# Attention planned with zero-padded key and query stacks, value products of two query tiles, and four fixed pairs of accumulator banks

## The chip, the cores and the metric

The kernel runs on one core of a Trainium2 chip, one launch, inputs and outputs in device memory. The metric is the device time of one execution in microseconds (us). PE is TensorE (PEld its weight loads), DVE VectorE, ACT ScalarE, POOL GpSimd, SP the queue that issues most transfers. PSUM, where matmuls write, has 8 banks of 512 fp32 columns.

## What is computed

Two transformer-like layers over 512 latent and 128 context tokens, model width 1024. A layer is a modulated RMSNorm, one input projection, three groups of heads side by side (a bidirectional RG-LRU, grouped-query attention "G" with 8 heads, differential attention "D" with 4 heads), an output projection with a gated residual, then a second norm and a gated MLP with a width-3 convolution. The part that matters here:

```python
def _gqa_attend(q, k, v):                # 8 query heads, 2 key/value heads, head width 64
    s = einsum('bqhgd,bkhd->bhgqk', qblk, k) * scale
    p = softmax(s)                       # latent queries see 128 context + 512 latent keys
    return einsum('bhgqk,bkhd->bqhgd', p, v)

def _diff_attend(q, k, v, lam):          # 4 heads, two 32-wide components each
    s = einsum('bqhcd,bkhcd->bchqk', qblk, k) * scale
    p = softmax(s)
    att = p[:, 0] - lam * p[:, 1]
    return einsum('bhqk,bkhd->bqhd', att, v)
```

## The kernel before

Engines run their own instruction streams in program order, with semaphores between them; the order of each stream is fixed when the program is written out. Weights come in fp32 and are split into a rounded high part and a remainder (`split_next`: one ACT copy, one DVE subtraction); projections are three matmuls per tile (`mm3`, L344 to L346).

Two things set the order. `Flow` holds pieces of work by a time at which they become due and writes them out while matmuls go by. `Plan` writes out the attention stage of a layer: `plan_attention` makes a list of tasks with an engine, an assumed duration, a key, needs and counted rooms (3 score buffers `ps` of two banks, 2 single banks `pb`, 10 slots `tp`), and `Plan.run` steps a clock and writes the task with the smallest key that can start. Keys and the order of units come from the table `PLAN`, one entry per layer.

A layer's order: projections of q (`evac_gq`), of k, v and D's q (`evac_kvdq`), of D's k and v (`evac_dkdv`), then the two 128-wide tiles of the RG-LRU gate (`m` = 2 and 3, tiles `lacc`, L344 to L346 with 320 columns), then the plan. While the last ones run, `Flow` writes out context attention (`ctx_stage` L1034, `ctx_norm` L1056 to L1063, `ctx_T` L1071), the RG-LRU's gate product (L686) with its split `mix_out` (ACT L639, DVE L640), and the five stacks of D's first key pair.

A **stack** (`d_stack`) is what D's score matmul needs of one token tile: for four heads, high, high and low part side by side (3 x 32 = 96 columns). POOL rounds the high part (L349), DVE makes the low part (`lo`, L905), PE transposes it (`tr`, L910, tile `dT`), DVE copies it to `dks` or `dqs` in two halves (`out`, L914). A layer has 18: five keys and four queries for each of two head pairs. The plan writes 13, `d_stack_flow` the first five.

The plan's work for one unit (one head, 128 queries): scores on PE (L1147 and L1148 for G, L1152 for D), maximum on DVE (`nm`, L1158), exponential on ACT (L1162), reciprocal on DVE (L1167), scaling on POOL (L1173), for D a combination on DVE (L1177), transposes on PE (L1182, `PT`), their copy on ACT (L1187), and for every second unit the value product on PE (L1205, context part L1209, tile `PV`) with a copy on ACT (L1221). Between them PE runs the modulation products of later layers (`ada_gen`, L487), whose 1 MB of weights per piece SP loads. 48 units, 24 value products a layer.

`psum_mode` closes the PSUM pools of a stage and opens those of the next: 8 single banks outside the plan, 3 doubles and 2 singles in it.

Of the kernel before, what the change touches and what calls it, by code (L numbers as in the profile page):

```python
# [11 lines left out]
F32 = mybir.dt.float32  # L12
# [22 lines left out]
CX = (3000, 6500, 4000, 3000, 6000, 12000, 8000)  # L35
FIN = 7000
NP = (1250, 4000, 950, 1700)
PLAN = [dict(units="GDGDGGGGDGGGGDGGGDGGDDGGGDGGDGDDGGGGDDGGDDGGGGDG",
             G=(9, -21, 59, -142, -12, -22, 57, -93),
             D=(7, 28, 94, -471, 19, 10, -62, 241),  # L40
             ada=(131, -55, 4800), stacks=(2, 116, -14)),
        dict(units="GGGGGGDGGGDGGDGGDGDDGGGDGGDGGDGDDDGDGDGGGGDGDGGG",
             G=(-28, -30, -9, 36, -2, -50, 265, 122),
             D=(-18, 54, 54, -325, 3, -201, 99, -124),
             ada=(102, -48, 7800), stacks=(9, 164, 20))]
DT = 1500
# [47 lines left out]
class Plan:  # L94
# [3 lines left out]
    LAT = 180  # L98

    ROOM = dict(ps=3, pb=2, tp=10, sm=14, st=2, pt=5)  # L100

    def __init__(self, fl):
        self.fl, self.room, self.tasks = fl, dict(self.ROOM), []

    def task(self, eng, dur, key, fn, deps=(), take=None, give=None, cond=None, after=(), extra=()):
        t = dict(eng=eng, dur=dur, key=key, fn=fn, deps=list(deps), take=take or {}, give=give or {}, cond=cond,
                 after=list(after), extra=list(extra), end=None, n=len(self.tasks))
        self.tasks.append(t)
        return t

    def run(self):
        now, free, gifts = 0.0, {}, []
        left = sorted(self.tasks, key=lambda t: (t["key"], t["n"]))
        while left:
# [4 lines left out]
            started = False  # L119
            for t in left:  # L120
                if free.get(t["eng"], 0) > now:
                    continue
                if any(d["end"] is None or d["end"] + (0 if d["eng"] == t["eng"] else self.LAT) > now for d in t["deps"]):
                    continue
                if any(d["end"] is None or d["end"] + lag > now for d, lag in t["after"]):
                    continue
                if any(self.room[k] < n for k, n in t["take"].items()) or (t["cond"] and not t["cond"]()):
                    continue
                for k, n in t["take"].items():
# [1517 lines left out]
```

## Time and profile before

| | |
|---|---|
| median of 3 runs | 1640.56 us (1638.94 to 1643.58) |
| the profiled execution's own time | 1643.37 us |
| its span | 1641.6 us |
| PE busy, share of the span | 97% |
| DVE, ACT, POOL busy | 58%, 44%, 21% |
| scores of layer 0 start / first product after its attention | 179.81 / 306.18 us |
| the same in layer 1 | 984.92 / 1102.90 us |

Times in the trace are us from the start of the span. A row of the order of time gives start, duration and, in brackets, how long the engine was idle before it and what it waited for. The duration of a matmul row is longer than the distance to the next, because matmuls overlap in the engine; the distance between starts is what one costs.

### The profile page before, as it was taken

What the parts mean: (1) busy time and instruction counts of PE and PEld (TensorE: products, weight loads), DVE (VectorE), ACT (ScalarE), POOL (GpSimd) and SP (SyncE); (2) the same over time, 40 slices, a digit from 0 to 9 for tenths busy, and PEclk for the clock granted to TensorE, in tenths of its full rate; (3) what the DMA queues carried; (4) which work ended last, traced back from release to release, by engine and by line L of the source; (5) the groups of instructions that cost most, each with busy time, mean ns of one, the idle gap of its engine ahead of it and who ended that gap; (6) DMA issues with size and microseconds to landing.
All of it is one profiled execution on the core that took longest, in us unless ns stands there. A gap on an engine that the chain in (4) does not pass through costs nothing. (4 is left out here: it accounts for less than half of the span.)

```text
span 1641.6 us, 25381 instructions
## 1 busy us (share of the span) xinstructions
PE 1594.2 (97%) x10070; PEld 1393.8 (85%) x10070; DVE 945.0 (58%) x1548; ACT 726.3 (44%) x1500; POOL 344.8 (21%) x746
## 2 busy tenths in 40 slices
PE   6999899999999999999999999999999999999998
PEld 4778677789999889999887777777899998899986
DVE  5787777465555434555477777865655553355544
ACT  4745677634333212333247357884433331133331
POOL 5162233122111000110052513420411100011101
PEclk9999999999999999999999999999999999999999
DMA  9222465411313221222212214442112232121212
GB/s 331 69 86 78 142 218 208 156 52 53 102 52 108 98 77 52 78 78 90 90 41 71 75 58 155 136 162 102 52 52 86 69 129 78 52 78 54 101 65 90
DMA packets 99435, 161.04 MB, mean 98 GB/s; under 512 B 10670, under 2 KB 69222, under 8 KB 94196
## 3 DMA queue, kind: packets, MB, share of 16 engines
q1 hardware_dynamic: 98068, 158.00, 28.8%
q8 instruction: 79, 1.29, 0.3%
q0 software_dynamic: 1040, 1.14, 0.2%
q14 instruction: 40, 0.33, 0.1%
q10 hardware_dynamic: 208, 0.28, 0.0%
HBM read 155.95 MB, written 3.44 MB: 97 GB/s over the span
## 5 line engine op out<-in xcount | busy, mean ns | idle before, releaser
L330 DVE TENSOR_TENSOR wl<-raw,wh 128x1024 fp32r<-128x1024 f32 x180 | 219.9, 1227 | 410.1 <-ACT wh L329 409.1
L345 PE MATMUL uacc<-hl,wh 128*128 128x320 f32 (+2 forms) x1408 | 437.4, 311 | 0.8 <-DVE hl L574 0.5
L344 PE MATMUL uacc<-hh,wh 128*128 128x320 f32 (+2 forms) x1408 | 435.9, 310 | 0.0
L346 PE MATMUL uacc<-hh,wl 128*128 128x320 f32 (+2 forms) x1408 | 434.2, 308 | 0.2 <-DVE wl L330 0.2
L329 ACT ACTIVATE wh<-raw 128x1024 fp32r<-128x1024 f32 x180 | 189.6, 1059 | 180.3 <-PE tacc L346 148.6
L346 PEld LDWEIGHTS uacc<-hh,wl 128*128 128x128 f32 x1408 | 265.6, 189 | 0.7 <-DVE wl L330 0.7
L345 PEld LDWEIGHTS uacc<-hl,wh 128*128 128x128 f32 x1408 | 264.5, 188 | 1.7 <-DVE hl L574 1.6
L344 PEld LDWEIGHTS uacc<-hh,wh 128*128 128x128 f32 x1408 | 264.7, 188 | 0.3
L344 PE MATMUL tacc<-wh,g 128*128 128x512 f32 x440 | 174.2, 396 | 0.0
L345 PE MATMUL tacc<-wl,g 128*128 128x512 f32 x440 | 173.8, 395 | 0.0
L346 PE MATMUL tacc<-wh,g 128*128 128x512 f32 x440 | 173.3, 394 | 0.0
L1365 POOL TENSOR_SCALAR ca<-u,fcol 128x642 f32<-128x642 f32 x44 | 39.1, 889 | 416.7 <-issue 243.4
L1158 DVE TENSOR_REDUCE nm<-S 128x1 f32<-128x640 f32 x128 | 102.9, 819 | 31.8 <-PE S L1152 16.8
L1162 ACT ACTIVATE P<-S,nm 128x640 f32<-128x640 f32 x128 | 101.2, 793 | 35.0 <-DVE nm L1158 27.4
L1173 POOL TENSOR_SCALAR P<-P,den 128x640 f32<-128x640 f32 x96 | 78.9, 825 | 177.6 <-DVE den L1167 101.3
L1361 ACT ACTIVATE u<-uacc 128x192 f32<-128x192 f32 (+1 forms) x88 | 29.1, 331 | 183.9 <-PE uacc L346 183.9
L346 PEld LDWEIGHTS tacc<-wh,g 128*128 128x128 f32 x440 | 82.6, 188 | 20.0
L344 PEld LDWEIGHTS tacc<-wh,g 128*128 128x128 f32 x440 | 82.6, 188 | 19.6
L345 PEld LDWEIGHTS tacc<-wl,g 128*128 128x128 f32 x440 | 82.7, 188 | 19.1
L344 PE MATMUL acc<-wh,hh 128*128 128x512 f32 x240 | 97.4, 406 | 0.0
L345 PE MATMUL acc<-wl,hh 128*128 128x512 f32 x240 | 95.9, 399 | 0.0
L346 PE MATMUL acc<-wh,hl 128*128 128x512 f32 x240 | 95.7, 399 | 0.0
(291 smaller groups left out, 2673.2 us busy)
## 6 DMA issues: line engine op xcount, KB each, us to landing
raw<-in_ffn_w_up_dram SPq DMA_DIRECT2D x44, 1024.0 KB, 5.1
raw<-in_ada_w_dram SPq DMA_DIRECT2D x40, 1024.0 KB, 4.9
raw<-in_ffn_w_down_dram SPq DMA_DIRECT2D x20, 1024.0 KB, 5.0
raw<-in_w_in_dram SPq DMA_DIRECT2D x16, 1024.0 KB, 8.4
araw<-in_ada_w_dram SPq DMA_DIRECT2D x16, 512.0 KB, 9.6
raw<-in_w_out_dram SPq DMA_DIRECT2D x8, 1024.0 KB, 5.2
gates<-gate SPq DMA_DIRECT2D x8, 512.0 KB
x<-in_x_sample_dram SPq DMA_DIRECT2D x4, 512.0 KB
```

The lines of the kernel that those rows point to most:

```text
L329: act.activation(out=wh, in_=raw, func=ACTF.Copy)
L330: dve.tensor_tensor(out=wl, in0=raw, in1=f32(wh), op=ALU.subtract)
L344: pe.matmul(out, lhsT=lh, rhs=rh, start=start, stop=False)
L345: pe.matmul(out, lhsT=lh, rhs=rl, start=False, stop=False)
L346: pe.matmul(out, lhsT=ll, rhs=rh, start=False, stop=stop)
L1158: dve.tensor_reduce(out=box["nm", c], in_=view(c), op=ALU.max, axis=AX.XY, negate=True)
L1162: act.activation(out=box["P"][c].rearrange("p (a b) -> p a b", a=2), in_=view(c), func=ACTF.Exp, bias=box["nm", c], accum_out=box["den"][: ...
L1173: pool.tensor_scalar(out=P[-1], in0=P[-1], scalar1=den[:, 1 + comps:2 + comps], scalar2=0.0, op0=ALU.mult, op1=ALU.add)
L1361: act.activation(out=u[:, 1 + cut:1 + L], in_=acc[1][:, 0:L - cut], func=ACTF.Copy)
L1365: pool.tensor_scalar(out=out, in0=u[:, 1:1 + n], scalar1=wcol(1), scalar2=wcol(3), op0=ALU.mult, op1=ALU.add)
```

## The change

- `psum_mode` no longer closes and opens pools. Four pairs of banks are taken once; `ps` takes one of the first three pairs, `pb` a bank (the last pair only, inside the plan). Which one is free is decided while the program is written out, by whether anything still refers to it; the least recently used is taken.
- Stacks are padded to 128 columns with a POOL memset of zeros; score matmuls of D run with 128 rows, transposes give 128 rows.
- All 18 stacks are tasks of the plan; `d_stack_flow` and its spacing rule are gone.
- A value product covers two query tiles: 40 matmuls (44 with the context) into one bank, and one copy of 256 or 384 columns; 12 a layer.
- The RG-LRU gate's halves are copied as each half ends (`lru_in`), and `mix_out` after it is due 12000 ns later, not 800. The second D context stage is due 2500 ns sooner (`CX`).
- `Plan.run` keeps a queue per engine and steps to the next event; new lags, durations and tables.

```diff
-CX = (3000, 6500, 4000, 3000, 6000, 12000, 8000)
+CX = (3000, 4000, 4000, 3000, 6000, 12000, 8000)
...
-PLAN = [dict(units="GDGDGGGGDGGGGDGGGDGGDDGGGDGGDGDDGGGGDDGGDDGGGGDG",
-             G=(9, -21, 59, -142, -12, -22, 57, -93),
-             D=(7, 28, 94, -471, 19, 10, -62, 241),
-             ada=(131, -55, 4800), stacks=(2, 116, -14)),
...
-DT = 1500
+PLAN = [dict(units="GDGGGDDGGDGGGGDDGGDGDGGGGDDGDGGGGGDGDDGDGDGGGGGG",
+             G=(-52, -319, -4222, 739, -24, -2061, 630, -1312),
+             D=(66, -829, -2569, -782, 139, 2157, -2109, -894),
+             ada=(214, 341, 3600), stacks=(-166, 98, -236, -24),
+             scale=(0.9965, 1.0396, 0.9868, 1.4475), lat=(109, 317)),
+        dict(units="GGGGDGDDGGGDGGGGDDGGGGGGGGGDGGDDDGDGGGGGDGDDDGDG",
...
-    def stacks(pos, jp, which, prev):
+    def stacks(pos, jp, which, prev, room=[]):
         ends = []
...
-            t = plan.task("pe", 230, key, f[2], [t], take=dict(pb=1))
-            ends.append(plan.task("dve", 700, key, f[3], [t], give=dict(pb=1, tp=1, st=1)))
+            t = plan.task("pe", 240, key, f[2], [t], take=dict(pb=1))
+            ends.append(plan.task("dve", 700, key, f[3], [t] + room, give=dict(pb=1, tp=1, st=1)))
         return ends

-    q0 = stacks(places[0], 0, "q", [])
+    k0 = stacks(places[3], 0, "k", [])
+    q0 = stacks(places[0], 0, "q", k0[-1:])
+
     k1 = stacks(places[1], 1, "k", q0[-1:])
     q1 = stacks(places[2], 1, "q", k1[-1:])
...
-        need = [] if kind == "G" else (k1 + q1 if p else q0)
+        need = [] if kind == "G" else (k1 + q1 if p else q0 + k0)
...
-        if not e:
-            pair[kind] = t
+        ready[kind].append(t)
+        if not (e and q % 2):
             continue
         f, ends, mix = values(kind, p, q), q == 3, kind == "G"
-        t = plan.task("pe", 1590 if ends else 1310, key + pr[6], f["mm"], [t, pair[kind]], take=dict(pb=1), give=dict(pt=1))
-        t = plan.task("act", 270 if ends else 170, key + pr[7], f["out"], [t], take=dict(tp=1 if mix and q == 0 else 0),
+        t = plan.task("pe", 2740 if ends else 2550, key + pr[6], f["mm"], ready[kind], take=dict(pb=1), give=dict(pt=2))
+        ready[kind] = []
+        t = plan.task("act", 360 if ends else 260, key + pr[7], f["out"], [t], take=dict(tp=1 if mix and q == 1 else 0),
                       give=dict(pb=1))
...
-    psum, mode = ctx.enter_context(ExitStack()), {}
+
+
+    pairs_ = ctx.enter_context(tc.tile_pool(name="acc", bufs=4, space=bass.MemoryType.PSUM))
+    bank_of = [pairs_.tile([128, 1024], F32, tag="acc", name="acc") for _ in range(4)]
+    held, used, turn = [None] * 8, [0] * 8, [0]
+
+    def take(banks, ap):
+        turn[0] += 1
+        for b in banks:
+            held[b], used[b] = [ap], turn[0]
+        return ap
...
+    def ps(name):
+        p = min((p for p in range(3) if idle(2 * p) and idle(2 * p + 1)), key=lambda p: max(used[2 * p:2 * p + 2]))
+        return take((2 * p, 2 * p + 1), bank_of[p][:, 0:1024])
+
+    def pb(name, dt=F32):
+        free = [b for b in range(8) if idle(b)]
+        if paired[0]:
+            free = [b for b in free if b >= 6]
+        b = min(free, key=lambda b: used[b])
+        ap = bank_of[b // 2][:, b % 2 * 512:b % 2 * 512 + 512]
+        return take((b,), ap.bitcast(dt) if dt != F32 else ap)
+
+    paired = [False]

     def psum_mode(double, single):
-
...
-        def lru_in(m, acc):
+        def lru_in(m, acc, b=None):
...
-                gg = tslot("lrug", T)
-                for b in range(2):
-                    act.activation(out=gg[:, b * CH:b * CH + CH], in_=acc[b][:, 0:CH], func=ACTF.Gelu_apprx_tanh)
+                if not b:
+                    lru["g"] = tslot("lrug", T)
+                gg = lru["g"]
+                act.activation(out=gg[:, b * CH:b * CH + CH], in_=acc[b][:, 0:CH], func=ACTF.Gelu_apprx_tanh)
...
                     dve.tensor_tensor(out=gg, in0=gg, in1=lru["S"][:, c], op=ALU.mult)
-                    fl.add(800, lambda: mix_out(c, gg))
+                    fl.add(12000, lambda: mix_out(c, gg))

...
-        def d_stack(df, dest, c0, order, jp):
-
...
+            pool.memset(f32(st[:, :, 3]), 0.0)
             round_pool(st[:, :, his[0]:his[1] + 1:step], d3.unsqueeze(2).to_broadcast([128, 4, 2, 32]))
             box = []

@@ -907,33 +948,15 @@
             def tr():
                 box.append(pb("dT", F32R))
                 for h in range(4):
-                    pe.transpose(box[0][0:96, h * 128:h * 128 + 128], st[:, h].rearrange("p s d -> p (s d)"), identr)
+                    pe.transpose(box[0][:, h * 128:h * 128 + 128], st[:, h].rearrange("p s d -> p (s d)"), identr)
...
             def out():
                 for e in range(2):
-                    dve.tensor_copy(out=dest[e][0:96, :, c0:c0 + 128],
-                                    in_=f32(box[0][0:96, e * 256:e * 256 + 256].rearrange("p (h c) -> p h c", h=2)))
-                pending[jp] -= 1
+                    dve.tensor_copy(out=dest[e][:, :, c0:c0 + 128],
+                                    in_=f32(box[0][:, e * 256:e * 256 + 256].rearrange("p (h c) -> p h c", h=2)))
+                box.clear()
...
-        for args in stack_args(0, "k"):
-            fl.add(CX[4], lambda args=args: d_stack_flow(1500, *args), 0, "st")
...
-            lru_in(m, acc)
+                lru_in(m, acc, c)
...
-            c0, nn = q * 128, 256 if q == 3 else 128
+            c0, nn = (q - 1) * 128, 384 if q == 3 else 256
...
-                out, PT = pb("PV"), PTs[kind, p, q]
+                out = pb("PV")
                 box.append(out)
-                for k in range(5):
-                    for e in range(2):
-                        pe.matmul(out[64 * e:64 * e + 64, 0:128], lhsT=V(e, k), rhs=PT[:, k, e * 128:e * 128 + 128],
-                                  start=(k == 0), stop=(k == 4), tile_position=(0, 64 * e))
+                for z in range(2):
+                    PT = PTs[kind, p, q - 1 + z]
+                    for k in range(5):
+                        for e in range(2):
+                            pe.matmul(out[64 * e:64 * e + 64, z * 128:z * 128 + 128], lhsT=V(e, k),
+                                      rhs=PT[:, k, e * 128:e * 128 + 128], start=(k == 0), stop=(k == 4), tile_position=(0, 64 * e))
```

The first place is PE's row of layer 0 where the gate's last products end and the scores begin. `lacc` (in the change every PSUM tile is called `acc`) are the gate's products, `dT` stack transposes, `cPTp` the context's. Before:

```order
L345 MATMUL lacc<-hl,wh 128x320
L346 MATMUL lacc<-hh,wl 128x320
L910 MATMUL dT<-identr,ds 96x128 x4
L344 MATMUL lacc<-hh,wh 128x320
L345 MATMUL lacc<-hl,wh 128x320
L346 MATMUL lacc<-hh,wl 128x320
L344 MATMUL lacc<-hh,wh 128x320
L345 MATMUL lacc<-hl,wh 128x320
L346 MATMUL lacc<-hh,wl 128x320
L910 MATMUL dT<-identr,ds 96x128 x4
L1071 MATMUL cPTp<-ident,cP 128x128 x2
L1147 MATMUL S<-kk,qa 128x320
```

and now, the same place and the first scores:

```order
L382 MATMUL acc<-hh,wl 128x320
L1094 MATMUL acc<-ident,cP 128x128 x2
L1170 MATMUL acc<-kk,qa 128x320
L1171 MATMUL acc<-kl,qa 128x320
L1170 MATMUL acc<-kk,qa 128x320
L1171 MATMUL acc<-kl,qa 128x320
L1170 MATMUL acc<-kk,qa 128x320
L1171 MATMUL acc<-kl,qa 128x320
L1170 MATMUL acc<-kk,qa 128x320
L1171 MATMUL acc<-kl,qa 128x320
L951 MATMUL acc<-identr,ds 128x128 x4
```

No stack transpose stands among the gate's products any more; the first comes after two units of scores.

The second place is DVE's row at the same time: `ds` are low parts of stacks, `dks` their copies, `crd` and `cP` the second D context stage, `lrug` and `mix` the RG-LRU's product and its split, `nm` the maxima. Before:

```order
L640 TENSOR_TENSOR mix<-lrug,mix 128x640
L914 CAST dks<-dT 96x2x128 x2
L905 TENSOR_TENSOR ds<-db,ds 128x4x32 x2
L914 CAST dks<-dT 96x2x128 x2
L1056 RECIPROCAL crd<-cden 128x4
L1059 TENSOR_TENSOR crd<-crd,neglam 128x1 x2
L1061 TENSOR_TENSOR cP<-cP,crd 128x512
L1063 TENSOR_TENSOR cP<-cP 128x2x128
L914 CAST dks<-dT 96x2x128 x2
L905 TENSOR_TENSOR ds<-db,ds 128x4x32
L914 CAST dks<-dT 96x2x128 x2
L686 TENSOR_TENSOR lrug<-lrug,lruS 128x640
```

and now:

```order
L1086 TENSOR_TENSOR cP<-cP 128x2x128
L946 TENSOR_TENSOR ds<-db,ds 128x4x32
L726 TENSOR_TENSOR lrug<-lrug,lruS 128x640
L1181 TENSOR_REDUCE nm<-acc 128x1 x3
L955 CAST dks<-acc 128x2x128 x2
L946 TENSOR_TENSOR ds<-db,ds 128x4x32
L1191 RECIPROCAL den<-den 128x1
L1181 TENSOR_REDUCE nm<-acc 128x1 x2
L677 TENSOR_TENSOR mix<-lrug,mix 128x640
L955 CAST dks<-acc 128x2x128 x2
L1181 TENSOR_REDUCE nm<-acc 128x1
L946 TENSOR_TENSOR ds<-db,ds 128x4x32 x2
```

The stacks' low parts and copies now stand between the first maxima, and both splits of the RG-LRU come after the first maxima instead of ahead of them.

The third place is PE's row at the end of layer 1's attention (`PT` transposes of units, `PV` value products, `adaT` a modulation transpose, `tacc` the output projection). Before:

```order
L1182 MATMUL PT<-ident,P 128x128 x15
L1205 MATMUL PV<-PT,va 64x128 x4
L1205 MATMUL PV<-PT,vb 64x128 x6
L1209 MATMUL PV<-vb 64x128 x2
L1182 MATMUL PT<-ident,P 128x128 x5
L506 MATMUL adaT<-ident,arow 128x128 x4
L1205 MATMUL PV<-PT,va 64x128 x20
L1209 MATMUL PV<-cPTg,va 64x128 x2
L344 MATMUL tacc<-wh,mix 128x512
```

and now:

```order
L1206 MATMUL acc<-ident,P 128x128 x25
L543 MATMUL acc<-ident,arow 128x128 x4
L1206 MATMUL acc<-ident,P 128x128 x5
L1232 MATMUL acc<-PT,va 64x128 x20
L1236 MATMUL acc<-cPTg,va 64x128 x2
L1232 MATMUL acc<-PT,va 64x128 x4
L1232 MATMUL acc<-PT,vb 64x128 x6
L1232 MATMUL acc<-PT,va 64x128 x4
L1232 MATMUL acc<-PT,vb 64x128 x6
L1236 MATMUL acc<-vb 64x128 x2
L380 MATMUL acc<-wh,mix 128x512
```

Six units' transposes now come together, then two value products with no transposes between them. Over both layers, groups of value products with other work between them go from 46 to 23.

## Rows read from the trace of the kernel before

**Rows 1.** The page's busy times of the whole span.

```profile
PE 1594.2 (97%) x10070; PEld 1393.8 (85%) x10070; DVE 945.0 (58%) x1548; ACT 726.3 (44%) x1500; POOL 344.8 (21%) x746
```

**Rows 2.** Busy us per engine in a stretch; the number after POOL's count is TensorE's granted clock.

```profile
160.00:180.00 20.00, 16.61 (x119) 15.37 (x118) 13.89 (x41) 9.91 (x26) 2.37 (x4) 0.91 0.16 54
179.80:306.00 126.20, 124.18 (x1192) 90.05 (x1192) 92.37 (x200) 95.82 (x208) 44.82 (x59) 1.00 0.60 207
```

**Rows 3.** Order of time on PE, layer 0, end of the projections.

```profile
170.41 0.31 PE L345 MATMUL lacc<-hl,wh 128*128 128x320 f32 x1
170.55 0.30 PE L346 MATMUL lacc<-hh,wl 128*128 128x320 f32 x1
173.35 0.63 PE L910 MATMUL dT<-identr,ds 128*96 128x128 f32 x4 [2.49 <-DVE ds L905]
...
174.42 0.47 PE L346 MATMUL lacc<-hh,wl 128*128 128x320 f32 x1
174.69 0.47 PE L344 MATMUL lacc<-hh,wh 128*128 128x320 f32 x1
...
179.81 0.38 PE L1147 MATMUL S<-kk,qa 128*128 128x320 f32 x1 [0.70 <-DVE dks L914]
```

**Rows 4.** The same on PE, layer 1.

```profile
978.35 0.45 PE L910 MATMUL dT<-identr,ds 128*96 128x128 f32 x4 [2.49 <-DVE ds L905]
```

**Rows 5.** Order of time on DVE, layer 0, same place.

```profile
171.52 0.83 DVE L640 TENSOR_TENSOR mix<-lrug,mix 128x640 fp32r<-128x640 f32 x1 [2.69 <-ACT mix L639]
...
172.93 0.48 DVE L905 TENSOR_TENSOR ds<-db,ds 128x128 fp32r<-128x128 f32 x2
```

**Rows 6.** Order of time on PE: value products, alone and in succession.

```profile
286.18 1.31 PE L1205 MATMUL PV<-PT,va 128*64 128x128 f32 x20
287.42 0.77 PE L1182 MATMUL PT<-ident,P 128*128 128x128 f32 x5
...
304.10 0.61 PE L1205 MATMUL PV<-PT,va 128*64 128x128 f32 x8
304.53 0.82 PE L1205 MATMUL PV<-PT,vb 128*64 128x128 f32 x12
305.19 0.39 PE L1209 MATMUL PV<-vb 128*64 128x128 f32 x4
```

**Rows 7.** Order of time on PE: waits after the first scores.

```profile
183.86 0.41 PE L1147 MATMUL S<-kk,qa 128*128 128x320 f32 x1 [0.74 <-ACT P L1162]
...
988.97 0.41 PE L1147 MATMUL S<-kk,qa 128*128 128x320 f32 x1 [0.81 <-ACT P L1162]
```

**Rows 8.** Order of time on DVE: a stack's copy and the next instruction.

```profile
189.01 0.75 DVE L914 CAST dqs<-dT 96x256 fp32r<-96x256 f32 x2
189.69 0.82 DVE L1158 TENSOR_REDUCE nm<-S 128x1 f32<-128x640 f32 x1
```

**Rows 9.** Groups in layer 0's attention: busy us, mean ns of one, idle before.

```profile
L1158 DVE TENSOR_REDUCE nm<-S 128x1 f32<-128x640 f32 x64 | 51.3, 819 | 16.1 <-PE S L1152 9.4 <-PE S L1148 6.4
L1187 ACT ACTIVATE PT<-PT 128x640 f32<-128x640 f32 x48 | 32.6, 704 | 6.2 <-PE PT L1182 5.8
L1221 ACT ACTIVATE mixf<-PV 128x128 f32<-128x128 f32 x12 | 3.3, 276 | 1.1 <-PE PV L1205 0.9
L1221 ACT ACTIVATE mixf<-PV 128x256 f32<-128x256 f32 x4 | 1.5, 382 | 0.5 <-PE PV L1209 0.5
```

**Rows 10.** Groups on POOL over the whole span: a memset.

```profile
L416 POOL MEMSET blk<- 128x128 f32 x1 | 0.3, 306 | 0.0
```

**Rows 11.** Order of time on DVE: a stack's low part.

```profile
991.77 0.81 DVE L905 TENSOR_TENSOR ds<-da,ds 128x128 fp32r<-128x128 f32 x1
```

**Rows 12.** Order of time on POOL, same moment: four scalings.

```profile
991.63 3.18 POOL L1173 TENSOR_SCALAR P<-P,den 128x640 f32<-128x640 f32 x4 [1.24 <-DVE den L1167]
```

**Rows 13.** All instructions on tiles ds: idle us before them, times.

```profile
  DVE dqs L914: 0.4, 1
```

**Rows 14.** Order of time on PE: the first product after layer 0's attention.

```profile
306.18 0.50 PE L344 MATMUL tacc<-wh,mix 128*128 128x512 f32 x1 [0.60 <-ACT dn L1221]
```

More of the change, by code (lines that the diff above doesn't have):

```diff
@@ L1 @@
 import math
+import sys
 from contextlib import ExitStack
@@ L109, in task, with due @@
         return t
+    def due(self, t):
+        at = 0.0
+        for d, lag in [(d, 0 if d["eng"] == t["eng"] else self.late(d["eng"])) for d in t["deps"]] + t["after"]:
+            if d["end"] is None:
+                return None
+            at = max(at, d["end"] + lag)
+        return at
     def run(self):
-        now, free, gifts = 0.0, {}, []
-        left = sorted(self.tasks, key=lambda t: (t["key"], t["n"]))
-        while left:
+        now, free, gifts = 0.0, dict(pe=0.0, act=0.0, dve=0.0, pool=0.0), []
+        order = sorted(self.tasks, key=lambda t: (t["key"], t["n"]))
+        queues = {e: [t for t in order if t["eng"] == e] for e in free}
+        while any(queues.values()):
             for g in [g for g in gifts if g[0] <= now]:
@@ L118, in run @@
                     self.room[k] += n
[L119 to L121 removed]
+            started, later = False, [g[0] for g in gifts]
+            for eng, queue in queues.items():
+                if free[eng] > now:
+                    later.append(free[eng])
                     continue
[L123 to L129, printed above, removed]
[L130 to L139 removed]
@@ new lines, in run @@
+                for t in queue:
+                    at = self.due(t)
+                    if at is None:
+                        continue
+                    if at > now:
+                        later.append(at)
+                        continue
+                    if any(self.room[k] < n for k, n in t["take"].items()):
+                        continue
+                    for k, n in t["take"].items():
+                        self.room[k] -= n
+                    t["fn"]()
+                    t["end"] = free[eng] = now + t["dur"]
+                    for e, off, dur in t["extra"]:
+                        free[e] = max(free[e], now + off) + dur
+                    if t["give"]:
+                        gifts.append((t["end"] + self.late(eng), t["give"]))
+                    queue.remove(t)
+                    started = True
+                    break
@@ L140, in run, with plan_attention @@
             if not started:
-                now += 20.0
-                self.fl.step(20.0)
+                step = max(1.0, min(later) - now)
+                now += step
+                self.fl.step(step)
         self.length = now
-def plan_attention(plan, par, ngen, unit, values, stack, ada, split, ready):
+def plan_attention(plan, par, ngen, unit, values, stack, ada, split):
     units, (a0, an, gap), places = par["units"], par["ada"], par["stacks"]
-    def stacks(pos, jp, which, prev):
+    def stacks(pos, jp, which, prev, room=[]):
@@ L1102, in mixer @@
                 lru_in(m, first[m])
+        del first[:]
         rope_tables_()
```

98 lines of the change are left out of this document (39 added, 59 removed).

## The prediction

> **What bounds the kernel now.** I read the page's busy times first, then windows by stage, then the order of time on PE around every wait, and went to the other engines only where a wait of PE names them. PE is busy for 97% of the span [rows 1], so a change can only pay by taking work from PE or by taking away one of its few waits. The windows say where those are. In layer 0's attention PE is busy for 124.18 of 126.20 us, at a granted clock of 1.00, while DVE, ACT and POOL stand at 92.37, 95.82 and 44.82 us [rows 2]: nearly packed, with some 2 us to gain. The 20 us just before it are another matter: PE 16.61 us, mean clock 0.91 [rows 2].
>
> There the order of time shows two waits. At 170.86 PE stops for 2.49 us, until the low part of a key stack is there, and at 179.11 for 0.70 us ahead of the first scores, for the copies of the last stacks [rows 3]. Layer 1 has the same pair: 2.49 us at the same place [rows 4], and 0.70 again ahead of the scores at 984.92. What is late is seen on DVE: it sat for 2.69 us on the split `mix` at L640, which needs ACT's half of it, and the low part of the stack (172.93) stood behind that split in DVE's queue [rows 5]. Behind PE's stop the gate's products start 0.27 us apart, where they were 0.14 apart ahead of it [rows 3]: the lower of the clock's two levels (1.2 against 2.4 GHz), for a few us.
>
> **The change part by part.**
>
> *The waits ahead of the scores.* Now no stack transpose stands among the gate's products, and the splits `mix` come after the first maxima (the first and second order). The low part that PE waited for is gone from the place, and so are the copies ahead of the first scores, which are G's and need only `qa`, `kk` and `kl`, ready long before. What could be late next are the context transposes `cPTp`; their inputs are made by the stage that `CX` brings 2.5 us forward, and the splits no longer stand ahead of them. So I take the whole: 2 x (2.49 + 0.70) = 6.4 us. Bounds: 4.9 us, if the 0.70 stays in both layers as another wait, and 6.4.
>
> *The half-rate stretch.* It followed directly on the stop, and with no stop I see nothing that would bring it about. Its price by the window: 20 us at 0.91 are 20 x 0.09 = 1.8 us short of full clock; not all of that held PE's work, since 3.4 of the 20 us were idle. I take 1.4 a layer, 2.8 us for both (layer 1's trace has the same spacing after its stop). Bounds 0, if another idle stretch brings it back, and 3.6.
>
> *The stacks.* The five that were ahead of the plan are now in it; their transposes are PE's in either place, so PE's sum doesn't change. Rows of 128 instead of 96 don't make a transpose or a score product longer: matmuls are priced here by the columns streamed, and those stay. The shape 128x320 among rows [rows 3] is what a D score becomes, and nothing on the page charges rows. The 36 memsets cost POOL at most 36 x 0.31 = 11 us by the one memset of 128x128 [rows 10]; POOL works for 45 of 126 us in attention [rows 2], so I put them at 0. Without that cover each would delay its stack by 0.31 us, which matters only where a D score waits for it.
>
> *Value products.* Groups of them with other work between them go from 46 to 23. Twenty records alone cost 1.24 us between starts (286.18 to 287.42); the 20 from 304.10 behind another set cost 1.09 (to 305.19) [rows 6]. So each merged pair saves 0.15 us, 23 x 0.15 = 3.4 us. Bounds: 0, if the extra is one of waiting and not of the switch; 6, if the group's other side is counted as well. ACT makes 24 copies fewer: two of 276 ns against one of 382 [rows 9], 24 x 0.17 = 4.1 us, but ACT has 30 us to spare in each attention [rows 2]: 0 on the path. The price is a later start: a value product waits for four units, not two, and holds more `PT`. PE has other units to do meanwhile.
>
> *End of attention.* The first output product waited 0.60 us for the copy of the last value product [rows 14], and about half a microsecond in layer 1. It used a newly opened pool; with kept banks it needs only `mix`. The third order ends on such a product as before, so the copy is still needed for the later products: I take 0.5 us in all, bounds 0 and 1.1.
>
> *What the start of the scores pays.* Before the first D score the changed order of layer 0 puts on DVE 14 maxima, 9 pairs of stack copies, 9 low parts and the two splits. By the rows: 14 x 0.82 [rows 9] + 9 x 0.68 [rows 8] + 9 x 0.24 + 2 x 0.83 [rows 5] = 21.4 us and a dozen small reciprocals, against an estimated 22 us of PE's work up to there (14 score sets of four products 0.14 apart are 7.8; nine stack transposes, ten unit transposes and six modulation pieces the rest, by their spacing in the trace). Before, there were six maxima and four pairs in that place. Two engines equally loaded for 22 us and chained through three score buffers don't stay packed: PE waited 0.74 and 0.81 us for ACT's exponential there even at the lighter load [rows 7], ACT being behind DVE's maxima. Walking both orders by hand I find 1.3 us more in layer 0 and 2 in layer 1: +3.5 with rounding. Bounds 1 and 8.
>
> *The end of layer 1.* Six unit transposes now follow each other (third order). ACT's copy is 704 ns each [rows 9], the five products of a set some 0.55 by my estimate: 6 x 0.15 = 0.9, and ahead of them ACT is already behind: +1.0. Bounds 0 and 2.
>
> **Sum.** -6.4 - 2.8 - 3.4 - 0.5 + 3.5 + 1.0 = -8.6 us. The profiled execution took 1643.37 us (span 1641.6, and 1.8 around it), 2.8 above the median of the runs. From it the sum gives 1634.8; from the median 1640.56 it gives **1632.0 us**, which I forecast. Outside attention and the 20 us ahead of it the orders on all engines agree, so nothing more is due there.
>
> **The rivals.** Less than 0.3% (4.9 us) is about what a measurement of this kernel can't tell from no change.
>
> *A, the gain is deeper.* The new tables (lags, scales, units) were set for a planner that steps to events, and may take the 2 us of waits inside each attention away, and the load at the start may be hidden by ACT's and DVE's slack. Then +4.5 becomes 0 and up to 4 more go: -8.6 - 4.5 - 1 = -14, 1626.5 us. For it: 30 us of slack on each of the other engines [rows 2]. Against it: the load at the start is real in the order.
>
> *B, the stack work gives the gain back.* Per layer five stacks move into attention, 5 x (0.24 + 0.68) = 4.6 us of DVE, in its fullest stretch. And low parts grow there: one took 0.81 us [rows 11], not 0.24 [rows 5], while POOL ran its scalings, four of which last 3.18 us [rows 12]. Nine of them stretched by 0.57 are 5 us more of DVE a layer, in the 22 us where it has none to spare. If 2.8 of these 5 us reach PE in each layer, the sum is -8.6 + 5.6 = -3, 1637.6 us. The Trainium skill, page "SBUF — State Buffer", section "Who interferes with whom", says that a DVE instruction with two SBUF inputs contends with a GpSimd instruction that reads SBUF, and not with one that only writes it. By that rule the low part, with both inputs in SBUF, is held up by scalings but not by the new memsets; the two rows agree.
>
> *C, slower: the bank of the stacks.* In the plan `pb` has two banks, and modulation pieces hold one for long. Through the other go 18 stack transposes a layer and the value products, each held until its copy is done. DVE does the stacks' copy, and it is queued behind maxima. PE stands at each transpose, in order, with everything behind it. To end slower than before by 0.3% this must cost 8.6 + 4.9 = 13.5 us, 0.38 us for each of 36 transposes. Against it: the 26 that were already in the plan cost PE hardly anything, the waits named for copies of a previous stack sum to 0.4 us [rows 13]; a copy takes 0.75 us [rows 8] and would have to be late by half its length each time. 1645 us and more.
>
> *Does it do what it says?* The moved stacks and the merged products stand in the order, so a plain no change needs B.
>
> **How the numbers follow.** Forecast 0.58, A 0.17, B 0.17, C 0.08. Forecast's own range 1627 to 1635.5: the gains at their best ends with the losses at their least reach some 5 us below 1632, and half of what the losses can grow by some 3.5 above it. The 8 in 10 reaches into A (1626.5 and some below) and through B: **1624 to 1640**, outside of which lie C and the far end of A. Faster by over 0.3% means below 1635.7: forecast and A, 0.75; same 0.17 (B); slower 0.08 (C).
>
> **What the profile of the changed kernel would show.** Right: no wait of 2.49 us among the gate's products and no 0.27 spacing there in either layer; the scores of layer 0 start 5 us or so sooner, near 174.5; PE waits for ACT's exponentials and for stack copies within the first 25 us of each attention, together 2 to 3 us a layer; value products come in runs of 40 at 0.055 us a record; the transposes at the end of layer 1 wait for ACT. Wrong, upwards: waits of PE for copies `dks` and `dqs` all through attention (C), low parts of 0.8 us in the first 25 us with PE idle behind them (B), or a clock below 1.00 in attention. Wrong, downwards: first 25 us of attention with PE waiting under 1 us (A). It would be wrong altogether if some stage outside attention changed its time by more than 2 us, since there nothing was moved.

## The result, and the profile after

The changed kernel takes 1766.79 us (median of 4 runs, 1763.84 to 1769.68), the one before 1639.75 us in the same session: a ratio of 1.0765, 95% interval 1.0749 to 1.0781. That is 127 us slower, against 8.6 us faster as forecast.

The page's busy line of the changed kernel answers to [rows 1]:

```profile
PE 1625.2 (92%) x10070; PEld 1408.5 (80%) x10070; DVE 943.9 (53%) x1548; ACT 725.6 (41%) x1476; POOL 350.4 (20%) x782
```

The span is 1765.2 us, 123.6 more. PE's matmuls are as many as before, but it is busy 31.0 us longer (1625.2 against 1594.2) and idle 92.6 us longer. So there is no new work on PE: it waits, and its records have become longer.

The next view answers where. It is the windows by stage, before first, then the changed kernel; the stages run to the first scores of layer 0, to the first PE instruction behind its last value product, to the first scores of layer 1, to the same place behind its attention, and to the end. (In layer 0 of the changed kernel, and of most runs made from it, that instruction is a modulation transpose; here it starts at 340.8 us, the output projection 0.4 us later.) Columns as in [rows 2].

```profile
0.00:179.80 179.80, 155.21 (x888) 125.78 (x889) 127.42 (x288) 97.83 (x219) 65.14 (x110) 0.98 0.41 131
179.80:306.20 126.40, 124.20 (x1193) 90.07 (x1193) 92.57 (x200) 96.02 (x209) 44.82 (x59) 1.00 0.60 207
306.20:984.90 678.70, 669.42 (x3805) 602.99 (x3806) 370.42 (x549) 262.19 (x534) 125.27 (x302) 0.99 0.23 76
984.90:1102.90 118.00, 115.55 (x1124) 88.28 (x1124) 90.83 (x196) 95.31 (x208) 43.20 (x59) 1.00 0.44 148
1102.90:1641.60 538.70, 529.84 (x3061) 486.73 (x3061) 263.79 (x319) 174.98 (x332) 66.36 (x216) 1.00 0.24 79
```

```profile
0.00:204.30 204.30, 162.52 (x868) 125.71 (x869) 120.63 (x272) 96.65 (x216) 64.21 (x109) 0.98 0.35 115
204.30:340.80 136.50, 124.87 (x1211) 92.57 (x1209) 95.30 (x211) 96.05 (x199) 48.77 (x78) 1.00 0.56 190
340.80:1068.60 727.80, 683.76 (x3790) 610.52 (x3790) 366.75 (x536) 261.94 (x532) 122.56 (x301) 0.98 0.22 71
1068.60:1195.50 126.90, 116.65 (x1147) 91.39 (x1144) 97.11 (x211) 94.35 (x196) 49.61 (x78) 1.00 0.41 138
1195.50:1765.20 569.70, 537.41 (x3063) 488.30 (x3061) 264.14 (x318) 176.56 (x334) 65.26 (x216) 0.99 0.22 74
```

The two attentions, which the change rewrote, account for 19 us of the loss (136.5 - 126.4 and 126.9 - 118.0). The other 105 us lie outside them: 24.5 ahead of the first scores, 49.1 between the attentions, 31.0 after the second one. Apart from the last 20 us ahead of each attention the order of PE's instructions is the same there as before. The last stage is the plainest: the same 3061 weight loads, 31 us more.

The list of waits of the changed kernel, for PE (sum, how often, the longest):

```profile
PE acc L380 <- ACT u L1388: 12.9, 22, 0.6
PE acc L380 <- DVE res L1313: 10.3, 13, 0.9
PE acc L586 <- DVE res L1313: 9.8, 4, 4.0
PE acc L380 <- ACT cP L1062: 8.3, 4, 3.2
PE acc L380 <- ACT hf L595: 6.3, 3, 2.3
```

None of these is in the list of before. They are many and mostly short: a first product of a new tile waits for a copy of an earlier one. In all PE's rows show 145 waits, 130.9 us together, where before they show 42 with 38.0 us. L1388 copies the last 128 columns of an MLP accumulator (L1386 and L1387 the rest). One of the 22, as the order of time shows it on PE and then on ACT:

```profile
1327.80 0.31 PE L382 MATMUL acc<-hh,wl 128*128 128x320 f32 x1
1328.70 0.42 PE L380 MATMUL acc<-hh,wh 128*128 128x320 f32 x1 [0.59 <-ACT u L1388]
```

```profile
1328.15 0.33 ACT L1387 ACTIVATE u<-acc 128x192 f32<-128x192 f32 x1 [1.11 <-PE acc L382]
1328.37 0.27 ACT L1388 ACTIVATE u<-acc 128x128 f32<-128x128 f32 x1
```

PE finishes a bank, ACT copies it, and PE, which goes on to another bank, starts 0.90 us after its last product started, instead of 0.15. The bank it goes to is not the one that ACT copies. What the two banks share is the pair: `bank_of` holds four tiles of 1024 columns, and `pb` gives out halves of them. In the built program every wait names the instruction that it waits for, so the banks on both sides can be read there. Counted are the waits that a matmul of PE carries itself and that guard a bank (the awaited instruction reads PSUM and makes none of the matmul's inputs); some more stand in instructions of their own ahead of a matmul and are left out:

```
                     same bank   other half of the pair   another pair
before                     294                        0              3
changed kernel             173                      165              0
```

All 35 waits of L380 for L1388 are of the second kind: into bank 5 it waits until bank 4 is read, for instance, or into bank 6 until bank 7 is. Before, a bank that was taken by itself was a tile by itself, so nothing tied two such banks together.

The Trainium skill, page "PSUM — Partial Sum Buffer", section "PSUM bank collisions raise a hardware error", asks for a guard by bank and quadrant, and lets two engines go undisturbed in different banks. The traces agree on different banks: in e5_halves_far below PE fills banks while others are being copied, and the 704 products shown there wait for 0.0 us in all. No run here has two engines in one bank at once, so the rest of the rule isn't tested. The guard by pair is the program's, not the chip's.

Some of the longer waits also bring the lower clock. At the start of layer 0's MLP (a product into bank 5 waits until DVE has read normed tiles, L597, from bank 4) PE stands for 3.11 us, after eight transposes. The products that follow come at 0.28 to 0.32 us, those ahead of it 0.18 apart, and the granted clock of 430.3 to 433.3 us is 0.55, near the lower of its two levels (0.5), where 415 to 427 us had 1.00:

```profile
425.37 0.34 PE L381 MATMUL acc<-hl,wh 128*128 128x384 f32 x1
425.55 0.33 PE L382 MATMUL acc<-hh,wl 128*128 128x384 f32 x1
425.72 0.66 PE L586 MATMUL acc<-ident,xn 128*128 128x128 f32 x4
426.55 0.66 PE L586 MATMUL acc<-ident,xn 128*128 128x128 f32 x4 [0.17 <-POOL xn L580]
430.32 0.48 PE L380 MATMUL acc<-hh,wh 128*128 128x384 f32 x1 [3.11 <-DVE hf L597]
430.60 0.51 PE L381 MATMUL acc<-hl,wh 128*128 128x384 f32 x1
430.91 0.53 PE L382 MATMUL acc<-hh,wl 128*128 128x384 f32 x1
431.23 0.53 PE L380 MATMUL acc<-hh,wh 128*128 128x384 f32 x1
```

So the 31.0 us by which PE's busy time grew are of two kinds. The granted clock of the whole span fell from 0.995 to 0.987, which by estimate is 0.008 x 1765 = 14 us. And at each stop the end of the last record, which the next product would have overlapped (0.31 us long at a distance of 0.15), counts as busy: 103 more stops at 0.16 are 16 us by estimate.

### The profile page after: what moved, and what is told of

Same layout as the page of the kernel before. It is cut to its first block, busy times and chain, and to the rows that moved or that the text cites. A ratio compares the mean times of both kernels' runs of the same rounds, so it can differ in the third digit from the quotient of the medians.

```text
span 1765.2 us, 25385 instructions
## 1 busy us (share of the span) xinstructions
PE 1625.2 (92%) x10070; PEld 1408.5 (80%) x10070; DVE 943.9 (53%) x1548; ACT 725.6 (41%) x1476; POOL 350.4 (20%) x782
## 5 line engine op out<-in xcount | busy, mean ns | idle before, releaser
L380 PE MATMUL acc<-hh,wh 128*128 128x320 f32 (+2 forms) x1536 | 485.5, 316 | 27.4 <-ACT u L1388 12.9
L381 PE MATMUL acc<-hl,wh 128*128 128x320 f32 (+2 forms) x1536 | 480.7, 313 | 0.4 <-DVE hl L611 0.3
L382 PE MATMUL acc<-hh,wl 128*128 128x320 f32 (+2 forms) x1536 | 478.8, 312 | 0.0
L380 PEld LDWEIGHTS acc<-hh,wh 128*128 128x128 f32 x1536 | 293.3, 191 | 35.7 <-ACT u L1388 18.6
L381 PEld LDWEIGHTS acc<-hl,wh 128*128 128x128 f32 x1536 | 293.4, 191 | 1.2 <-DVE hl L611 0.7
L382 PEld LDWEIGHTS acc<-hh,wl 128*128 128x128 f32 x1536 | 293.7, 191 | 0.2 <-DVE wl L366 0.2
L380 PE MATMUL acc<-wh,g 128*128 128x512 f32 x440 | 174.6, 397 | 8.8 <-DVE res L1313 7.1
L381 PE MATMUL acc<-wl,g 128*128 128x512 f32 x440 | 173.5, 394 | 0.0
L382 PE MATMUL acc<-wh,g 128*128 128x512 f32 x440 | 173.1, 393 | 0.0
L1181 DVE TENSOR_REDUCE nm<-acc 128x1 f32<-128x640 f32 x128 | 101.6, 818 | 26.3 <-PE acc L1171 14.7
L380 PEld LDWEIGHTS acc<-wh,g 128*128 128x128 f32 x440 | 82.6, 188 | 31.8 <-DVE res L1313 9.7
L380 PE MATMUL acc<-wh,hh 128*128 128x512 f32 x240 | 97.9, 408 | 10.0 <-ACT da L991 2.4
L382 PEld LDWEIGHTS acc<-wh,g 128*128 128x128 f32 x440 | 82.7, 188 | 19.4
```

The source lines that it names most:

```text
L380: pe.matmul(out, lhsT=lh, rhs=rh, start=start, stop=False)
L381: pe.matmul(out, lhsT=lh, rhs=rl, start=False, stop=False)
L382: pe.matmul(out, lhsT=ll, rhs=rh, start=False, stop=stop)
L1181: dve.tensor_reduce(out=box["nm", c], in_=view(c), op=ALU.max, axis=AX.XY, negate=True)
```

## The experiments

The theory (H in the expectations): a pair is one tile, dependencies are recorded by tile, and so a matmul into one half waits for the reader of the other half. Rivals: the new plan itself is slow (P), or the rule by which a bank counts as idle leaves too few to choose from (F). In the built programs of the changed kernel, e1_pools and e2_far_half all engines have the same instructions in the same order; only the PSUM tiles and the waits differ. Each run is measured against the kernel before on the same chip (its medians were 1643.0, 1642.0 and 1641.7 us in the three sessions).

**e1_pools.** The pools come back, all else stays changed.

```diff
-    pairs_ = ctx.enter_context(tc.tile_pool(name="acc", bufs=4, space=bass.MemoryType.PSUM))
...
+    psum, mode = ctx.enter_context(ExitStack()), {}
...
+    def ps(name, dt=F32):
+        return mode["ps"].tile([128, 1024], dt, tag="ps", name=name)
+    def pb(name, dt=F32):
+        return mode["pb"].tile([128, 512], dt, tag="pb", name=name)
```

> The changed kernel with one part undone: the PSUM pools are closed and opened per stage as before (8 single banks outside the plan, 3 doubles and 2 singles in it); padded stacks, plan, tables and merged value products stay. Theory H (a kept pair of banks is one tile, and the recorded dependencies go by tile: a matmul into one half waits for the engine that reads the other half): the whole loss of 127 us goes with the pairs, and what is left is what the prediction costed, 1632 us (1624 to 1640). Rival P (the new plan, with its stacks and merged products, carries a large part of the loss): the two attentions account for 18.6 us of the loss, so 1645 us or more. Rival F (too few free banks, since a bank that something still refers to isn't taken): like H here.

Measured: 1637.57 us, ratio 0.9973 (0.9963 to 0.9983). The whole loss went with the pairs; P is out. The rest of the change is a gain of 0.27%, half of the 0.5% that the sum had for it. F says the same here and is left to e2_far_half and e5_halves_far.

**e2_far_half.** One line of the changed kernel.

```diff
-        b = min(free, key=lambda b: used[b])
+        b = min(free, key=lambda b: (max(used[b // 2 * 2:b // 2 * 2 + 2]), used[b]))
```

> The changed kernel with one line changed: a single bank is taken not by its own age but by that of the later used half of its pair, so that the other half is one whose reader was done long ago where possible. The number of free banks and what refers to them are the same. Theory H: outside attention, where 105 of the 124 us were lost (24.5 before the first scores, 50.1 between the attentions, 30.4 after the second), most goes: some 80 of it, to 1685 us (1660 to 1705); inside attention only two halves of one pair are to be had, so its 18.6 us stay. Rival F (too few free banks): no change, 1767. Rival P: no change outside attention either.

Measured: 1683.49 us, ratio 1.0249 (1.0234 to 1.0263), 83 us less than the changed kernel. Waits for the other half still stand in the program, 135 of them, but most name readers that are done by then. From the second attention to the last product PE takes 530.1 us by the order of time, as before; the 22 waits for `u` and all but 1.8 us of those for `res` at L380 are gone. Of the 41 us that its trace still has above that of e1_pools, 18 lie between the attentions and 9 ahead of the first. Waits for context copies remain:

```profile
PE acc L380 <- ACT cP L1062: 9.2, 6, 1.7
PE acc L380 <- ACT cPTg L1096: 4.5, 2, 2.3
```

F is out for this part: neither the number of banks nor what holds them changed.

**e3_two_single.** The fourth pair becomes two tiles.

```diff
-    bank_of = [pairs_.tile([128, 1024], F32, tag="acc", name="acc") for _ in range(4)]
+    bank_of = [pairs_.tile([128, 1024], F32, tag="acc", name="acc") for _ in range(3)]
+    lone = [lone_.tile([128, 512], F32, tag="lone", name="lone") for _ in range(2)]
...
+        ap = lone[b - 6][:, 0:512] if b >= 6 else bank_of[b // 2][:, b % 2 * 512:b % 2 * 512 + 512]
```

> The changed kernel, but the fourth pair is two tiles of one bank each, which are recorded apart; the other three pairs stay, and banks are taken by the same rule. Theory H: in attention the single banks no longer depend on each other, so its 18.6 us go nearly whole (15); outside, two of eight banks are freed, a quarter of 105, 20 to 26 us: 1767 - 38 = 1729 (1715 to 1742). Rival F: 1767. Rival P (the plan's own waits): attention stays at 134.6 and 126.7 us from first scores to last value product, and the total within 1740 to 1767.

Measured: 1720.71 us, ratio 1.0476 (1.0459 to 1.0494). The direction and the size of the total hold. Inside attention the expectation was too high: layer 0's went from 136.5 to 130.0 us, layer 1's only from 126.9 to 125.9, 7.5 of the 15 us.

**e4_before_halves.** The kernel before, with halves of four tiles after layer 1's attention (the same references dropped as in the change, so that banks come free).

```diff
-        psum_mode(0, 8)
+        psum_mode(0, 8, l == 1)
...
+            b = min((b for b in range(8) if held[b] is None or sys.getrefcount(held[b][0]) <= 2), key=lambda b: used[b])
+            ap = mode["of"][b // 2][:, b % 2 * 512:b % 2 * 512 + 512]
```

> The kernel before, with one thing added: for the stage after layer 1's attention (output projection and MLP, 531 us), the 8 single banks are halves of four tiles of two banks, taken least recently used among those nothing refers to; all else as before. Theory H: that stage loses what it lost in the changed kernel, 30 us: 1670 us (1660 to 1676). Rival P: no plan is changed, so 1640. Rival F: like H here, its partner in the next comparison.

Measured: 1676.66 us, ratio 1.0208 (1.0191 to 1.0224), just above the expected range: 33.7 us for one stage, a little over the 31.0 that the changed kernel lost there. Three groups of PE in that stage, with the idle time ahead of them, now have the waits of the changed kernel; the first line is the first of these groups in the kernel before:

```profile
L344 PE MATMUL uacc<-hh,wh 128*128 128x320 f32 (+2 forms) x704 | 218.7, 311 | 0.0
L358 PE MATMUL acc<-hh,wh 128*128 128x320 f32 (+2 forms) x704 | 220.4, 313 | 9.2 <-ACT u L1382 7.0 <-DVE srow L1614 1.2 <-ACT hh L584 1.0
L358 PE MATMUL acc<-wh,g 128*128 128x512 f32 x220 | 87.4, 397 | 3.9 <-DVE res L1307 3.9
L564 PE MATMUL acc<-ident,xn 128*128 128x128 f32 x40 | 6.1, 303 | 4.9 <-DVE res L1307 4.9
```

**e5_halves_far.** The fourth kernel with the second's rule for taking a bank (the key of `min` alone).

> The fourth kernel (the one before with halves of four tiles in the stage after layer 1's attention, 1676.7 us against 1643.0) with the bank taken by the age of the later used half of its pair. The same eight banks, the same idleness. Theory H: the stage falls from 562.7 us back to about the 530.1 it had before: 1645 us (1640 to 1650). Rival F (the rule by which a bank counts as idle leaves too few): no change, 1676.

Measured: 1643.04 us, ratio 1.0004 (0.9995 to 1.0013). Halves of tiles, kept by the same rule of idleness, cost nothing that can be told from noise where the other half has long been read. That leaves F no room. The first group above, in this kernel:

```profile
L358 PE MATMUL acc<-hh,wh 128*128 128x320 f32 (+2 forms) x704 | 218.6, 311 | 0.0
```

**e10_far_single.** Both mendings of the second and third kernel in one.

> The changed kernel with both mendings at once: the fourth pair as two tiles of a bank each, and the other banks taken by the age of the later used half of their pair. Theory H: the second kernel (1683.5 us) still lost inside attention and between the attentions; with the single banks apart, layer 0's attention falls from 134.0 to 130 us as in the third kernel, layer 1's from 127.6 to 126, and some of the 18 us that the stage between them has above that of pools per stage goes too: 1672 us (1662 to 1679). If the two mendings touched the same waits only, 1683.

Measured: 1671.49 us, ratio 1.0183 (1.0168 to 1.0199). As expected, the second mending brings something beyond the first, but the two overlap: 83 and 46 us alone, 95 together. Still it is 34 us above e1_pools, half of that between the attentions (692.1 us against 676.2) and some 4 in each of them: three pairs are still tied.

The other runs are about the smaller terms. At the end of layer 0's attention e1_pools showed this on PE:

```profile
301.38 0.39 PE L1223 MATMUL PV<-vb 128*64 128x128 f32 x4
303.49 0.66 PE L530 MATMUL adaT<-ident,arow 128*128 128x128 f32 x4 [1.72 <-DVE arow L519]
304.59 0.47 PE L367 MATMUL tacc<-wh,mix 128*128 128x512 f32 x1 [0.44 <-DVE cm L533]
305.63 0.80 PE L368 MATMUL tacc<-wl,mix 128*128 128x512 f32 x1 [0.57 <-DVE wl L353]
306.22 0.63 PE L369 MATMUL tacc<-wh,mix 128*128 128x512 f32 x1
306.65 0.63 PE L367 MATMUL tacc<-wh,mix 128*128 128x512 f32 x1
```

The last modulation transpose has come to stand right ahead of the output projection. It needs `arow`, and DVE waits for the bias that SP loads for it:

```profile
302.75 0.69 DVE L519 TENSOR_TENSOR arow<-ada,abias 128x512 f32<-128x512 f32 x1 [6.18 <-DMA abias<-in_ada_b_dram]
```

Behind the stops the products are 0.43 us apart, against 0.23 from 309.15 on, and the granted clock of 304.5 to 309.2 us is 0.64: mostly the lower level again.

**e6_pools_ada.** e1_pools with one number.

```diff
-             ada=(214, 341, 3600), stacks=(-166, 98, -236, -24),
+             ada=(214, 341, 3300), stacks=(-166, 98, -236, -24),
```

> The first kernel (pools per stage, all else changed: 1637.6 us against 1643.0) with one number of layer 0's table changed, the spacing of modulation pieces 3600 to 3300, so that the last modulation transpose stands ahead of the last value product and not right ahead of the output projection. Theory G (the part of the forecast gain that the first kernel lacks, some 4 us, went into the waits of 1.72, 0.44 and 0.57 us at the end of layer 0's attention and into the half-rate products that follow them, 304.6 to 309.1): 1633.5 us (1631 to 1636). Rival Q (the reordered plan waits elsewhere instead): 1637.

Measured: 1633.52 us, ratio 0.9949 (0.9935 to 0.9963), as G has it, though the interval just touches that of e1_pools (0.9963 to 0.9983). Of the two traces the stretch from the first scores of layer 0 to those of layer 1 went from 803.0 to 799.6 us, 3.4 less. Ahead of it the two programs are the same, so the other 4.2 us by which the two traces differ there are not the edit's. The transpose now stands in front of the value products and waits for nothing, and the output projection starts at its usual spacing:

```profile
296.24 0.60 PE L530 MATMUL adaT<-ident,arow 128*128 128x128 f32 x4
296.77 0.66 PE L1219 MATMUL PV<-PT,va 128*64 128x128 f32 x8
...
299.99 0.50 PE L367 MATMUL tacc<-wh,mix 128*128 128x512 f32 x1 [0.59 <-ACT dn L1235]
300.32 0.39 PE L368 MATMUL tacc<-wl,mix 128*128 128x512 f32 x1
300.55 0.39 PE L369 MATMUL tacc<-wh,mix 128*128 128x512 f32 x1
```

**e7_before_mix.** The kernel before with one number.

```diff
-                    fl.add(800, lambda: mix_out(c, gg))
+                    fl.add(12000, lambda: mix_out(c, gg))
```

> The kernel before with one number changed: the RG-LRU's mix_out is due 12000 ns after its product, not 800. PE's order is the same. Theory of the prediction (the low part of a stack is late only because the split of mix stands ahead of it on DVE): the waits of 2.49 us at 173 and 978 us and the half rate behind them go, some 7 us of 1643, 1636 us (1634 to 1639). Rival: the low part is late with the next thing in DVE's queue, or the splits now delay the first maxima, 1641 or more.

Measured: 1636.08 us, ratio 0.9963 (0.9950 to 0.9976). The step of the prediction holds by itself: with the split out of DVE's way, the transposes that waited 2.49 us [rows 3] wait for nothing, those of the last stack wait 0.29, and the gate's products ahead of the scores keep their 0.15 us. The 0.70 stays:

```profile
172.69 0.41 PE L910 MATMUL dT<-identr,ds 128*96 128x128 f32 x4
...
174.34 0.45 PE L910 MATMUL dT<-identr,ds 128*96 128x128 f32 x4 [0.29 <-DVE ds L905]
174.62 0.41 PE L1071 MATMUL cPTp<-ident,cP 128*128 128x128 f32 x2
175.72 0.38 PE L1147 MATMUL S<-kk,qa 128*128 128x320 f32 x1 [0.69 <-DVE dks L914]
```

**e8_before_pv.** The kernel before, with value products of two query tiles.

```diff
-        if not e:
-            pair[kind] = t
+        ready_[kind].append(t)
+        if not (e and q % 2):
             continue
...
-            c0, nn = q * 128, 256 if q == 3 else 128
+            c0, nn = (q - 1) * 128, 384 if q == 3 else 256
...
+                for z in range(2):
+                    PT = PTs[kind, p, q - 1 + z]
```

> The kernel before with the value products of two query tiles merged, 12 a layer in place of 24, in the old plan and with its old tables (room for six PT in place of five). Theory of the prediction (each merge saves 0.15 us): 24 x 0.15 = 3.6 us less, 1639.5 us (1637 to 1642). Rival: the old tables were not set for it, products come later and hold banks longer, and the plan waits elsewhere: 1643 to 1650.

Measured: 1661.00 us, ratio 1.0113 (1.0096 to 1.0129). Both were wrong: 19 us slower, outside the rival's range too. The attentions grew from 126.4 and 118.0 to 138.7 and 126.3 us. Some of the new waits, in order of time:

```profile
218.53 0.77 PE L1183 MATMUL PT<-ident,P 128*128 128x128 f32 x5 [1.02 <-ACT P L1163]
220.54 0.76 PE L1183 MATMUL PT<-ident,P 128*128 128x128 f32 x5 [0.66 <-POOL P L1174]
237.71 0.77 PE L1183 MATMUL PT<-ident,P 128*128 128x128 f32 x5 [0.69 <-ACT P L1163]
```

In the second row PE comes to a unit's transposes before POOL has scaled its exponentials. In the first and third it waits for the score buffer that the transposes go into: an exponential (L1163) still reads scores from it. The tables of before were set for products of one tile; why exactly they fail with the merged ones was not pursued.

**e9_no_pad.** e6_pools_ada with stacks of 96 columns and no memset.

```diff
-            pool.memset(f32(st[:, :, 3]), 0.0)
...
-                Q, K = stacks[p, "q"][e][:, c], stacks[p, "k"][e][:, c]
+                Q, K = stacks[p, "q"][e][0:96, c], stacks[p, "k"][e][0:96, c]
```

> The sixth kernel (pools per stage, spacing 3300; 0.9949 of the one before) with the padding undone: stacks of 96 columns, no memset, score products of 96 rows; the same order of matmuls. The prediction's step (36 memsets on POOL cost nothing, and rows of a product aren't charged): the same ratio, 0.995 (0.993 to 0.997). Rival: the memsets hold up the stacks at the start of the scores, or a product of 128 rows is dearer, so that without them 2 us or more are gained, 0.9935 or less.

Measured: 1631.36 us, ratio 0.9941 (0.9929 to 0.9953). The interval overlaps that of e6_pools_ada; the difference of the two, 0.0008 or 1.3 us, is smaller than either is known to. The times can't tell the two apart, but they don't exclude the rival's 2 us either. The traces say more. A score product of D lasts 312 ns (median of 128) with 128 rows and with 96, so rows aren't charged. PE's listed waits in the first 25 us behind the first scores are 1.26 and 2.55 us by layer with the memsets, 0.68 and 2.51 without: a difference of 0.6 us at most.

## Why the prediction was wrong

**The step that failed** is its last sentence on the sum: "Outside attention and the 20 us ahead of it the orders on all engines agree, so nothing more is due there." The order of the instructions did agree. What an instruction waits for is not in the order, and that changed: 165 matmuls of PE now wait for the other half of their pair. The pairs of banks were costed in one term alone, the first product after attention (0.5 us); the price of 127 us for them stood in no term and in no rival. The list of what would show the prediction wrong did name it ("if some stage outside attention changed its time by more than 2 us"), and that is what the windows show.

**The sign.** The rivals that cost time (B and C) both lie inside attention. The measured time falls under C's words "1645 us and more", but only by luck: the attentions lost 19 us, the rest 105. Rival C, the bank of the stacks, had the right kind of mechanism (PE stands while a bank is being read) and the wrong bank: in the changed kernel copies of stacks delayed modulation pieces in the other half of their pair (L523 behind `dks` L955, 2.5 us by the list of waits), and stack transposes only once (1.0 us). B's long low parts are there, but few: in the first 25 us of attention in e1_pools one of eight in layer 0 and two of eight in layer 1 last over 0.8 us, where B had nine.

**The rest of the change**, without the pairs, was worth -4.4 us by the ratio of e1_pools (0.9973; its interval allows -2.8 to -6.1) where -8.6 was forecast, and these are its terms:

- The waits ahead of the scores and the half rate behind them (-6.4 and -2.8): confirmed in kind by e7_before_mix, -6.0 us alone. Of the four waits, the two of 2.49 us went. The two of 0.70 did not, which the lower bound of the term (4.9) allowed: in e1_pools the first scores wait 0.80 us for ACT's `lrug`.
- The merged value products: 40 records took 2.34 us in e6_pools_ada (292.21 to the next transposes at 294.55 us in its order of time), against 2 x 1.24 [rows 6], 0.14 a merge where 0.15 was taken. But e8_before_pv shows that there is a price in the plan around it, at least with tables set for single products, which the term left out with "PE has other units to do meanwhile".
- The start of the scores (+3.5): in the first 25 us the listed waits of PE in e1_pools sum to 1.30 us in layer 0 and 2.55 in layer 1, against 0.74 and 1.17 before. Counted in distances between starts, beyond the median of their kind, the growth is 1.3 and 2.0 us, as walked out.
- The first output product (-0.5): in the changed kernel that of layer 1 indeed waits for nothing (1195.51 us; 0.48 us before). In e1_pools, with its newly opened pool, the wait is back (0.59).
- The end of attention: the prediction looked at layer 1 and gave it +1.0, which did not come: in e1_pools 25 transposes take 2.79 us there and wait for nothing, as 15 took 1.78 before. It missed layer 0, where the modulation transpose ahead of the output projection costs what e6_pools_ada won back, some 4 us. With that the sum is nearly made up: e6_pools_ada is at -8.5 us (1642.0 to 1633.5) beside the forecast of -8.6. That they agree so closely is partly chance, since the interval reaches from -6 to -11 us and terms were off both ways.
- The memsets at nothing and the rows of a product: the traces of e9_no_pad bear the rows out (312 ns with either) and leave the memsets 0.6 us at most at the start of the scores.

**Open:** with separate single banks each attention still takes 3 to 5 us longer than with pools (130.0 and 125.9 against 126.8 and 121.3 us). The kept pairs are taken by the age of their taking while the program is written; that this picks a pair which is still being read is likely, but no run tells it. The full change turned back, the kernel before with pairs throughout, wasn't tried on the chip; only its last stage was.

## What to carry to other kernels

Compare what instructions wait for, not only their order: a change of how buffers are cut (one tile of two banks for two tiles of one) leaves every row of the order as it was and can still add a wait to a first product, as it did here in 165 places. Keep the tile as small as the unit that is filled and read by itself; if a larger one must be kept, take next the half whose partner was read longest ago (83 of 127 us came back by one line). And price a merge of instructions together with the planner around it: 3.4 us of saving cost 19 in a plan that was set for the unmerged ones.

## What the runs showed of the hardware

A short wait costs more than the list of waits says. In the changed kernel PE's idle time grew by 92.6 us, but its busy time by 31.0 with the same number of matmuls: a stop listed with 0.59 us put the next product 0.90 us behind the last instead of 0.15, so it cost 0.75. The other part of the 31.0 us are products at the lower of the clock's two levels behind longer stops (0.32 us apart for 0.18 behind a stop of 3.11 us, 0.43 for 0.23 behind the stops of 1.72, 0.44 and 0.57). Moving one transpose away from such a place brought some 4 us, where the waits listed there sum to 2.7; that it was more doesn't stand clear of noise, but the products behind them ran at half rate as well.
